# A bf16 matmul with bias and residual: load sizes of x and residual decoupled, weight loads on two queues, bias spread by a matmul

## The chip, the core and the metric

The kernel runs on one core of a Trainium2 chip. The core has five engines with queues of their own: TensorE (PE, matmul and transpose), VectorE (DVE), ScalarE (ACT), GpSimd (POOL) and SyncE (SP, which here only issues DMAs). An engine takes its instructions strictly in the order of its queue. DMAs are issued here from SP's queue and from ScalarE's, and 16 DMA engines carry them out. The metric is the device time of one execution in microseconds, lower is better.

## The reference

```python
batch, m, k, n = 16, 512, 1024, 768
# x: (16, 512, 1024), weight: (1024, 768), bias: (768,), residual: (16, 512, 768), all float32
def reference(x, weight, bias, residual):
    return (np.matmul(x, weight) + bias + residual).astype(np.float32)
```

In all 8192 rows of x are multiplied by one 1024 x 768 matrix. The kernel multiplies in bf16 and accumulates in float32. It reads 33.55 MB of x, 25.17 MB of residual and 3.15 MB of weights, and writes 25.17 MB.

## The kernel before, in words

The 8192 rows are cut into 64 row-tiles of 128 rows, counted by t. Two neighbouring row-tiles (SUB = 2) form a super s, and loads and stores go by super: one DMA brings x for 256 rows (1 MB, two rows of 4 KB, so 8 KB for each of 128 partitions), one the residual for 256 rows (768 KB), and one takes 256 rows of output away (768 KB). x, residual and output have five buffers each, so that five supers (ten row-tiles) can be in them.

Before the loop, `const` tiles are made: an identity for the transposes, the bias repeated over 128 partitions (`bias_bcast`, L102, a DMA that reads the same 3 KB for each partition), and the weights. Eight DMAs (L104), one for each slice k of 128 contraction rows, bring float32 weights into `w_stage`; VectorE casts each to bf16 in `w_sb` (L107, through the helper's L82). The bias DMA and the eight weight DMAs are all on ScalarE's queue, marked as of high priority.

A row-tile goes through these stages, each a function:

- `stage_load(s)` (L116): x and residual of a super are loaded from SP's queue (L120, L123), and GpSimd adds the bias to the residual in place (L127).
- `stage_a(t)` (L132): ScalarE casts 128 x 1024 of x to bf16 (`xb_tile`, L137 through L80). There are four such buffers.
- `stage_b(t)` (L140): TensorE transposes eight 128 x 128 blocks into PSUM (L146), VectorE copies them to `xt_tile` (L152 through L82).
- `stage_c(t)` (L155): 16 matmuls (L162), for each k one of 512 and one of 256 columns, accumulate in `psum_o`, of which there are three.
- `stage_d(t)` (L171): VectorE adds `psum_o` and the residual into `out_tile` (L176). After the second row-tile of a super, ScalarE's queue issues the store (L180).

The loop (L193) writes these down in the order load, a(t+2), b(t+1), c(t), d(t). The framework that builds the kernel puts each engine's instructions in order and inserts all waits: for data, for a buffer to come free, and for a DMA's completion semaphore to be free for use again. High priority moves instructions ahead in their queue.

Of the kernel before, what the change touches and what calls it, by code (L numbers as in the profile page):

```python
# [9 lines left out]


MM_DT = mybir.dt.bfloat16
SUB = 2
BIAS_MODE = "gpsimd"
WCV_ENGINE = "vector"
CONVERT_ENGINE = "scalar"
COPYBACK_ENGINE = "vector"
PIPE_AB = 2
X_BUFS = 5
RES_BUFS = 5  # L20
OUT_BUFS = 5
XB_BUFS = 4
XT_BUFS = 5
POUT_BUFS = 3
PTRANS_BUFS = 2
W_SPLIT = 4
W_PRIO_BUMP = 70


@with_exitstack  # L30
def kernel(
    ctx: ExitStack,
    tc: tile.TileContext,
    x: bass.AP,
    weight: bass.AP,
    bias: bass.AP,
    residual: bass.AP,
    out: bass.AP,
):
    nc = tc.nc  # L40
    P = 128
    FP32 = mybir.dt.float32
    BF16 = mybir.dt.bfloat16

    x2d = x.flatten_outer_dims()
    res2d = residual.flatten_outer_dims()
    out2d = out.flatten_outer_dims()
    M, K = x2d.shape
    Kw, N = weight.shape
    assert Kw == K  # L50
    n_k = K // P
    SUPER = SUB * P
    n_super = M // SUPER
    n_sub = n_super * SUB
    assert M % SUPER == 0

    x_sup = x2d.rearrange("(s p j) k -> s p j k", p=P, j=SUB)
    res_sup = res2d.rearrange("(s p j) n -> s p j n", p=P, j=SUB)
    out_sup = out2d.rearrange("(s p j) n -> s p j n", p=P, j=SUB)

    if N <= 512:
        n_chunks = [(0, N)]
    else:
        n_chunks = [(0, 512), (512, N - 512)]

    const = ctx.enter_context(tc.tile_pool(name="const", bufs=1))
    xin_pool = ctx.enter_context(tc.tile_pool(name="xin", bufs=1))
    xbf_pool = ctx.enter_context(tc.tile_pool(name="xbf", bufs=1))
    xt_pool = ctx.enter_context(tc.tile_pool(name="xt", bufs=1))
    res_pool = ctx.enter_context(tc.tile_pool(name="res", bufs=1))  # L70
    out_pool = ctx.enter_context(tc.tile_pool(name="outp", bufs=1))
    ptrans_pool = ctx.enter_context(tc.tile_pool(name="ptrans", bufs=1, space=bass.MemoryType.PSUM))
    pout_pool = ctx.enter_context(tc.tile_pool(name="pout", bufs=1, space=bass.MemoryType.PSUM))

    def rr_tile(pool, base, idx, nbufs, shape, dtype):
        return pool.tile(shape, dtype, name=base, tag=f"{base}{idx % nbufs}", bufs=1)

    def eng_copy(eng_name, out_ap, in_ap):
        if eng_name == "scalar":
            nc.scalar.copy(out=out_ap, in_=in_ap)  # L80
        elif eng_name == "vector":
            nc.vector.tensor_copy(out=out_ap, in_=in_ap)  # L82
        elif eng_name == "gpsimd":
            nc.gpsimd.tensor_copy(out=out_ap, in_=in_ap)
        else:
            nc.any.tensor_copy(out=out_ap, in_=in_ap)

    ident = const.tile([P, P], BF16, name="ident")
    make_identity(nc, ident)

    w_dram = weight.rearrange("(ko ki) n -> ki ko n", ki=P)
    w_sb = const.tile([P, n_k, N], MM_DT, name="w_sb")
    w_stage = const.tile([P, n_k, N], FP32, name="w_stage")

    with tc.high_priority():
        bias_bcast = const.tile([P, N], FP32, name="bias_bcast")
        bcast_ap = bass.AP(
            tensor=bias.tensor,
            offset=bias.offset,
            ap=[[0, P], bias.ap[0]],  # L100
        )
        nc.scalar.dma_start(out=bias_bcast, in_=bcast_ap)  # L102
        for k in range(n_k):
            nc.scalar.dma_start(out=w_stage[:, k, :], in_=w_dram[:, k, :])  # L104

    for k in range(n_k):
        eng_copy(WCV_ENGINE, w_sb[:, k, :], w_stage[:, k, :])  # L107

    x_tiles = {}
    res_tiles = {}  # L110
    out_tiles = {}
    xb_tiles = {}
    xt_tiles = {}
    psum_o_tiles = {}

    def stage_load(s):  # L116
        if s >= n_super:
            return
        x_tile = rr_tile(xin_pool, "x_tile", s, X_BUFS, [P, SUB, K], FP32)
        nc.sync.dma_start(out=x_tile, in_=x_sup[s])  # L120
        x_tiles[s] = x_tile
        res_tile = rr_tile(res_pool, "res_tile", s, RES_BUFS, [P, SUB, N], FP32)
        nc.sync.dma_start(out=res_tile, in_=res_sup[s])  # L123
        res_tiles[s] = res_tile
        bb = bias_bcast[:, None, :].to_broadcast([P, SUB, N])
        if BIAS_MODE == "gpsimd":
            nc.gpsimd.tensor_add(out=res_tile, in0=res_tile, in1=bb)  # L127
        else:
            nc.vector.tensor_add(out=res_tile, in0=res_tile, in1=bb)
        out_tiles[s] = rr_tile(out_pool, "out_tile", s, OUT_BUFS, [P, SUB, N], FP32)  # L130

    def stage_a(t):  # L132
        if t < 0 or t >= n_sub:
            return
        s, j = divmod(t, SUB)
        xb_tile = rr_tile(xbf_pool, "xb_tile", t, XB_BUFS, [P, K], BF16)
        eng_copy(CONVERT_ENGINE, xb_tile, x_tiles[s][:, j, :])  # L137
        xb_tiles[t] = xb_tile

    def stage_b(t):  # L140
        if t < 0 or t >= n_sub:
            return
        xb_tile = xb_tiles.pop(t)
        psum_t = rr_tile(ptrans_pool, "psum_t", t, PTRANS_BUFS, [P, n_k, P], BF16)
        for k in range(n_k):
            nc.tensor.transpose(  # L146
                out=psum_t[:, k, :],
                in_=xb_tile[:, ts(k, P)],
                identity=ident,
            )  # L150
        xt_tile = rr_tile(xt_pool, "xt_tile", t, XT_BUFS, [P, n_k, P], MM_DT)
        eng_copy(COPYBACK_ENGINE, xt_tile, psum_t)  # L152
        xt_tiles[t] = xt_tile

    def stage_c(t):  # L155
        if t < 0 or t >= n_sub:
            return
        xt_tile = xt_tiles.pop(t)
        psum_o = rr_tile(pout_pool, "psum_o", t, POUT_BUFS, [P, N], FP32)
        for k in range(n_k):  # L160
            for (n0, nl) in n_chunks:
                nc.tensor.matmul(  # L162
                    psum_o[:, n0:n0 + nl],
                    lhsT=xt_tile[:, k, :],
                    rhs=w_sb[:, k, n0:n0 + nl],
                    start=(k == 0),
                    stop=(k == n_k - 1),
                )
        psum_o_tiles[t] = psum_o

    def stage_d(t):  # L171
        if t < 0 or t >= n_sub:
            return
        s, j = divmod(t, SUB)
        psum_o = psum_o_tiles.pop(t)
        nc.vector.tensor_add(  # L176
            out=out_tiles[s][:, j, :], in0=psum_o, in1=res_tiles[s][:, j, :]
        )
        if j == SUB - 1:
            nc.scalar.dma_start(out=out_sup[s], in_=out_tiles.pop(s))  # L180

    next_load = [0]

    def ensure_loaded(s):
        while next_load[0] <= min(s, n_super - 1):
            stage_load(next_load[0])
            next_load[0] += 1

    ensure_loaded(max(1, (PIPE_AB - 1) // SUB + 1))
    for u in range(PIPE_AB):  # L190
        stage_a(u)
    stage_b(0)
    for t in range(n_sub):  # L193
        ta = t + PIPE_AB
        ensure_loaded(ta // SUB + 1)
        stage_a(ta)
        stage_b(t + 1)
        stage_c(t)
        stage_d(t)
# [30 lines left out]
```

## Time and profile before

| | us |
|---|---|
| median of 6 runs | 229.46 (229.14 to 229.60) |
| profiled execution | 229.34 |
| its span, first to last instruction | 227.6 |

| engine | busy us (share) | instructions |
|---|---|---|
| PE | 198.3 (87%) | 1536 |
| PE weight loads | 130.0 (57%) | 1536 |
| DVE | 108.9 (48%) | 136 |
| ACT | 67.8 (30%) | 65 |
| POOL | 110.7 (49%) | 38 |

The row of slices on the profile's page says how the engines' work lies over the 40 equal slices of the span, 5.69 us each: TensorE shows 0030 and then 9 until the end, the DMA engines' row shows 9 from the second slice to the 36th, then 4333. 87.68 MB were moved, 385 GB/s as a mean over the span. The granted TensorE clock was 0.994 of full speed. Transfers took, from issue to landing (medians): x 15.6 us, residual 14.9, output 8.6, weights 10.9, bias 6.8.

How to read it: a busy time is the sum of the durations of an engine's instructions; the chain of waits follows the last instruction back to what released it, step by step, and says which engine or DMA each stretch of the span belongs to. An idle time is given with a releaser, the engine or DMA whose event came last before the instruction started; where several events are waited for, the one named can be a bystander.

### The profile page before, as it was taken

The numbers are of one execution on the slowest core, as the hardware profiler recorded it, in microseconds if no ns is written. First come the engines' busy times: TensorE is split into PE (matmuls) and PEld (weight loads), VectorE is DVE, ScalarE is ACT, GpSimd is POOL, SyncE is SP. The second block draws the span as 40 slices with busy tenths as digits, with TensorE's granted clock in tenths as the row PEclk, the third lists the DMA queues.
The fourth block names the chain that finished last, engine by engine and source line by source line (L and its number), as shares of the span: only waits on it lengthen the run. The fifth ranks groups of instructions, "written<-read, shape, count | busy, mean of one in ns | idle before, by whom it ended". The sixth has DMA issues, their size and how long they took to land.

```text
span 227.6 us, 3719 instructions
## 1 busy us (share of the span) xinstructions
PE 198.3 (87%) x1536; PEld 130.0 (57%) x1536; DVE 108.9 (48%) x136; ACT 67.8 (30%) x65; POOL 110.7 (49%) x38
## 2 busy tenths in 40 slices
PE   0030499999999999999999999999999999999990
PEld 0020166666666666666666666666666666666660
DVE  0182635555444455554445555444455554444541
ACT  0080313333323333332233324233333332231000
POOL 1142876353666654165551666655555546459300
PEclk9999999999999999999999999999999999999997
DMA  6999999999999999999999999999999999994333
GB/s 202 404 407 425 415 421 343 372 419 420 424 429 419 427 419 428 424 423 426 425 423 426 419 429 420 426 422 420 425 420 427 424 421 422 425 381 185 141 140 138
DMA packets 15138, 87.68 MB, mean 385 GB/s; under 512 B 1680, under 2 KB 1680, under 8 KB 11024
## 3 DMA queue, kind: packets, MB, share of 16 engines
q1 hardware_dynamic: 9216, 58.72, 62.7%
q10 hardware_dynamic: 5904, 28.71, 30.6%
q8 instruction: 12, 0.20, 0.3%
q14 instruction: 6, 0.05, 0.1%
HBM read 62.26 MB, written 25.17 MB: 384 GB/s over the span
## 4 chain that ended last, share of the span: by engine, by line
PE 86%; DMA 9%; DVE 2%; ACTq 0%; issue 0%
PE psum_o L162 74%; PE psum_t L146 12%; DMA w_stage<-in_weight_dram 9%; DVE w_sb L82 1%; DVE out_tile L176 0%; DVE xt_tile L82 0%; ACTq L102 0%; ACTq L104 0%
## 5 line engine op out<-in xcount | busy, mean ns | idle before, releaser
L162 PE MATMUL psum_o<-w_sb,xt_tile 128*128 128x512 bf16 (+1 forms) x1024 | 178.7, 328 | 10.4 <-DVE xt_tile L82 10.4
L127 POOL TENSOR_TENSOR res_tile<-res_tile,bias_bcast 128x1536 f32<-128x1536 f32 x32 | 110.0, 3440 | 101.2 <-DMA res_tile<-in_residual_dram 91.6
L162 PEld LDWEIGHTS <-xt_tile 128*128 128x128 bf16 x1024 | 98.2, 98 | 70.1 <-DVE xt_tile L82 10.7
L176 DVE TENSOR_TENSOR out_tile<-psum_o,res_tile 128x768 f32<-128x768 f32 x64 | 61.3, 957 | 98.4 <-PE psum_o L162 56.6
L80 ACT CAST xb_tile<-x_tile 128x1024 bf16<-128x1024 f32 x64 | 66.5, 1045 | 127.0 <-PE psum_t L146 81.3
L146 PE MATMUL psum_t<-ident,xb_tile 128*128 128x128 bf16 x512 | 39.8, 222 | 13.7 <-ACT xb_tile L80 13.7
L146 PEld LDWEIGHTS <-xb_tile 128*128 128x128 bf16 x512 | 34.4, 99 | 21.9 <-ACT xb_tile L80 13.8
L82 DVE COPY xt_tile<-psum_t 128x1024 bf16<-128x1024 bf16 x64 | 43.4, 680 | 0.0
L82 DVE CAST w_sb<-w_stage 128x768 bf16<-128x768 f32 x8 | 9.4, 1184 | 16.0 <-DMA w_stage<-in_weight_dram 16.0
L80 ACT ACT_TABLE_LOAD x1 | 1.3, 1283 | 11.3 <-DMA w_stage<-in_weight_dram 11.3
masks.py:197 POOL MEMSET ident<- 128x128 bf16 x1 | 0.2, 204 | 0.3 <-POOLq L214 0.3
masks.py:199 POOL TENSOR_SCALAR_AFFINE_SELECT ident<-ident 128x128 bf16<-128x128 bf16 x1 | 0.3, 292 | 0.1
L214 POOL MEMSET const-float32-0.0<- 128x1 f32 x1 | 0.1, 98 | 0.2 <-issue 0.2
L214 POOL MEMSET const-bfloat16-1.0<- 128x1 bf16 x1 | 0.1, 102 | 0.0
L214 POOL MEMSET const-uint8-127<- 128x1 uint8 x1 | 0.1, 102 | 0.0
L214 POOL MEMSET const-float32-1.0<- 128x1 f32 x1 | 0.1, 98 | 0.0
## 6 DMA issues: line engine op xcount, KB each, us to landing
x_tile<-in_x_dram SPq DMA_DIRECT2D x32, 1024.0 KB, 15.6
res_tile<-in_residual_dram SPq DMA_DIRECT2D x32, 768.0 KB, 14.9
out_dram<-out_tile ACTq DMA_DIRECT2D x32, 768.0 KB, 8.6
w_stage<-in_weight_dram ACTq DMA_DIRECT2D x8, 384.0 KB, 10.9
bias_bcast<-in_bias_dram ACTq DMA_DIRECT2D x1, 384.0 KB, 6.8
```

What stands on the lines that cost most here:

```text
L80: nc.scalar.copy(out=out_ap, in_=in_ap)
L82: nc.vector.tensor_copy(out=out_ap, in_=in_ap)
L127: nc.gpsimd.tensor_add(out=res_tile, in0=res_tile, in1=bb)
L146: nc.tensor.transpose(out=psum_t[:, k, :], in_=xb_tile[:, ts(k, P)], identity=ident,)
L162: nc.tensor.matmul(psum_o[:, n0:n0 + nl], lhsT=xt_tile[:, k, :], rhs=w_sb[:, k, n0:n0 + nl], start=(k == 0), stop=(k == n_k - 1),)
L176: nc.vector.tensor_add(out=out_tiles[s][:, j, :], in0=psum_o, in1=res_tiles[s][:, j, :])
L214: nc = _bacc.Bacc("TRN2", target_bir_lowering=False, num_devices=1)
```

## The change

- x is loaded by four row-tiles (`XROWS` = 4: 2 MB for each DMA, 16 KB for each partition) into three buffers (12 row-tiles). The residual is still loaded by two row-tiles, now into six buffers, with counters of its own. The rows of a group of four are dealt to the partitions so that each partition holds four neighbouring rows.
- The output is stored by single row-tile: 64 stores of 384 KB in place of 32 of 768 KB, from eight buffers.
- Weight slices 4 to 7 are loaded from SP's queue with high priority, ahead of x; slices 0 to 3 from ScalarE's queue behind the bias. Casts of the weights move from VectorE to ScalarE. The matmuls take k in the order 4 to 7, 0 to 3.
- The bias is loaded as one row of 3 KB, cast to bf16, multiplied by a column of ones on TensorE (into the space of one of the `psum_o` tiles) and copied to `bias_bcast` by VectorE.
- Ahead of everything a two-element copy is put on ScalarE.

```diff
-SUB = 2
+XROWS = 4
+RES_ROWS = 2
-WCV_ENGINE = "vector"
+WCV_ENGINE = "scalar"
-X_BUFS = 5
-RES_BUFS = 5
-OUT_BUFS = 5
+X_BUFS = 3
+RES_BUFS = 6
+OUT_BUFS = 8
+W_SPLIT_ACT = 4
+K_ROTATE = 4
...
+    x_ld = x2d.rearrange("(S p j) k -> S p j k", p=P, j=XROWS)
+    res_4d = res2d.rearrange("(S p j) n -> S p j n", p=P, j=XROWS)
+    out_4d = out2d.rearrange("(S p j) n -> S p j n", p=P, j=XROWS)
...
+    k_order = [(K_ROTATE + i) % n_k for i in range(n_k)]
...
+    warm = const.tile([1, 2], FP32, name="warm")
+    nc.vector.memset(warm, 0.0)
+    nc.scalar.copy(out=warm, in_=warm)
...
     with tc.high_priority():
-        bias_bcast = const.tile([P, N], FP32, name="bias_bcast")
-        bcast_ap = bass.AP(
-            tensor=bias.tensor,
-            offset=bias.offset,
-            ap=[[0, P], bias.ap[0]],
+        for k in range(W_SPLIT_ACT, n_k):
+            nc.sync.dma_start(out=w_stage[:, k, :], in_=w_dram[:, k, :])
+
+    with tc.high_priority():
+        bias_row = const.tile([1, N], FP32, name="bias_row")
+        nc.scalar.dma_start(out=bias_row, in_=bias[None, :])
+        for k in range(W_SPLIT_ACT):
+            nc.scalar.dma_start(out=w_stage[:, k, :], in_=w_dram[:, k, :])
+
+    ones_col = const.tile([1, P], BF16, name="ones_col")
+    nc.vector.memset(ones_col, 1.0)
+    bias_row16 = const.tile([1, N], BF16, name="bias_row16")
+    nc.vector.tensor_copy(out=bias_row16, in_=bias_row)
+    bias_psum = pout_pool.tile([P, N], FP32, name="bias_psum", tag="psum_o0", bufs=1)
+    for (n0, nl) in n_chunks:
+        nc.tensor.matmul(
+            bias_psum[:, n0:n0 + nl],
+            lhsT=ones_col,
+            rhs=bias_row16[:, n0:n0 + nl],
+            start=True,
+            stop=True,
         )
-        nc.scalar.dma_start(out=bias_bcast, in_=bcast_ap)
-        for k in range(n_k):
-            nc.scalar.dma_start(out=w_stage[:, k, :], in_=w_dram[:, k, :])
+    bias_bcast = const.tile([P, N], FP32, name="bias_bcast")
+    nc.vector.tensor_copy(out=bias_bcast, in_=bias_psum)
...
+        out_tile = rr_tile(out_pool, "out_tile", t, OUT_BUFS, [P, N], FP32)
         nc.vector.tensor_add(
-            out=out_tiles[s][:, j, :], in0=psum_o, in1=res_tiles[s][:, j, :]
+            out=out_tile, in0=psum_o, in1=res_tile[:, t % RES_ROWS, :]
         )
-        if j == SUB - 1:
-            nc.scalar.dma_start(out=out_sup[s], in_=out_tiles.pop(s))
+        nc.scalar.dma_start(out=out_st_ap(t), in_=out_tile)
...
+    ensure_xloaded(0)
+    ensure_resloaded(1)
     for u in range(PIPE_AB):
         stage_a(u)
     stage_b(0)
     for t in range(n_sub):
         ta = t + PIPE_AB
-        ensure_loaded(ta // SUB + 1)
+        ensure_xloaded(ta // XROWS + 1)
+        ensure_resloaded(ta // RES_ROWS + 1)
         stage_a(ta)
         stage_b(t + 1)
         stage_c(t)
```

## The prediction

> **What bounds the kernel now.** I read the chain of waits first, then the busy shares by stretch, then the timelines of the start and of ScalarE. The chain, by line:
>
> ```profile
> PE 86%; DMA 9%; DVE 2%; ACTq 0%; issue 0%
> PE psum_o L162 74%; PE psum_t L146 12%; DMA w_stage<-in_weight_dram 9%; DVE w_sb L82 1%; DVE out_tile L176 0%; DVE xt_tile L82 0%; ACTq L102 0%; ACTq L104 0%
> ```
>
> So the run has two parts: a start that waits for the weights, and TensorE without a gap. Their border, in order of time:
>
> ```profile
> 10.80 12.21 DMA w_stage<-in_weight_dram
> 23.04 2.36 DVE w_sb L82
> 25.40 0.61 DVE xt_tile L82
> 26.05 4.79 PE psum_o L162 x16
> 30.84 0.45 PE psum_t L146 x8
> 31.29 2.60 PE psum_o L162 x16
> ```
>
> The last weight slice lands at 23.04, its cast takes 2.36, a copy 0.61, and the first output product starts at 26.05. From 31.29 each row-tile costs 2.60 + 0.45 = 3.05 us; 64 of them run to 222.37. Then come an add (0.96) and the last store, to 227.6. The stretches (columns: busy us of each engine, clock, DMA share, GB/s):
>
> ```profile
> 0.00:26.00 26.00, 1.98 (x16) 1.55 (x16) 10.00 (x10) 7.12 (x7) 7.65 (x9) 1.00 0.94 366
> ...
> 31.00:205.00 174.00, 174.00 (x1375) 114.92 (x1373) 89.02 (x115) 59.58 (x57) 91.47 (x27) 1.00 1.01 418
> 205.00:227.60 22.60, 17.34 (x128) 10.98 (x126) 9.23 (x12) 1.04 (x1) 7.49 (x3) 0.94 0.37 150
> ```
>
> TensorE is full from 31 to 205, at full clock, and **so are the DMA engines**. A row-tile moves 0.524 MB of x and 0.393 MB each of residual and output: 1.311 MB in 3.05 us is 430 GB/s, and 418 were moved. The kernel eats a stock of loaded rows all the way. An earlier start thus begins with a smaller stock.
>
> Where the stock gets short shows on ScalarE, late in the run:
>
> ```profile
> 166.29 1.05 ACT L80 CAST xb_tile<-x_tile 128x1024 bf16<-128x1024 f32 x1 [2.86 <-DVE out_tile L176]
> 168.48 1.04 ACT L80 CAST xb_tile<-x_tile 128x1024 bf16<-128x1024 f32 x1 [1.14 <-PE psum_t L146]
> 172.47 0.34 ACTq L180 DMA_DIRECT2D out_dram<-out_tile  x1
> 172.90 1.04 ACT L80 CAST xb_tile<-x_tile 128x1024 bf16<-128x1024 f32 x1 [3.38 <-DVE xt_tile L82]
> ```
>
> ScalarE stands still between 169.5 and 172.47, and the view blames VectorE, long done. The instruction records name the true cause: the 73 transfers share eight completion semaphores, and a transfer is issued only after the earlier user of its semaphore has landed. The store of 172.47 (rows 44, 45) uses that of the x load for rows 54, 55, and its count completes at 172.4. Stores at 160.13, 165.85, 178.46 and 184.60 match such landings too. So a store on ScalarE waits for x about ten rows ahead, and the casts queued behind it wait as well. TensorE feels nothing yet, since casts run six rows ahead of stores: the first store, after row 1, has eight casts before it.
>
> **The start, part by part.** The packet records give medians of 121, 234 and 309 ns for 3072, 6144 and 8192 bytes; the slope makes 16384 bytes 309 + 8192 x (75/2048) = 609 ns (estimate). Each transfer is 8 packets on each of 16 engines. In the first 12 us the two queues' packet counts run level (46 against 47 in the third and fourth us): packets alternate. That is why weights are late now: a 3 KB packet takes turns with an 8 or 6 KB one, and only five transfers of ScalarE's queue are in flight at first.
>
> *Split of the weights, ahead of x on SP.* The Trainium skill (DMA: Bandwidth & Descriptors, Issuing engines are not separate DMA queues) says that issuing on several engines saves issue time alone: four issues of 0.45 us, 1.8 us. The rows say more about this case, through order rather than rate: the slice landing at 17.6 took 1.0 us when ScalarE's queue ran alone, the one at 23.0 took 3.3 us beside x. With weights first on both queues nothing alternates with them: 64 packets per engine x 0.121 = 7.75, from the first packet at 1.75, and 1 us for the ramp (2.9 MB had moved by 10 us, about 1 us short of full rate): moved by 10.5, usable at 12.0 with 1.5 from last packet to landing. By the skill the weights would still end near 21; I take the rows.
>
> *Weight casts to ScalarE.* A 1024-element cast takes 1.045; 768 elements about 0.83 (between 0.78, in proportion, and 1.05). In slice order, five remain when slice 3 lands: 12.0 + 4.2 = 16.2. VectorE loses 9.4 us of casts off the later path, and the 2.36 on the chain with them. The early dummy copy brings the table load (1.28) forward under the weights. If x came sooner, the casts would be the wait.
>
> *x in 2 MB loads.* x0 follows the weights on SP: 8 x 0.609 = 4.87, moved at 15.4, landed at 16.9, just behind the casts. Then cast 1.05, a second cast 0.95 later to 18.9, its transposes 1.0 (the last pair took that), so **the first product starts at 20.0 instead of 26.05: 6.05 us gained**. The next x needs 1.57 MB of residual and 2.1 MB more, some 9 us: landed near 26, wanted near 30, hidden.
>
> *Bias by two matmuls, two small copies.* No row is near for one-row operands; by the 128-row ones they cost below 3 us, on idle engines behind a 3 KB load of about 3 us, with no residual before 18. Zero on the path; not below, since the broadcast load it replaces is 8 packets, 1 us of DMA, in the sum below. Rotation of k: all casts precede x, so zero. First product cold (4.79 against 2.60): kept; the transposes just before could save up to 1.5.
>
> *Granularity.* Per engine, x: 16 x 8 x 0.609 = 78.0 for 32 x 8 x 0.309 = 79.1; stores: 64 x 8 x 0.121 = 62.0 for 59.9; bias -1.0. Sum zero. Here a rule speaks against the change: the same page (Rules for kernel authors) wants 1 MiB or more per DMA, with 2.0 us fixed for each by its fit; 32 more stores would be 64 us if each paid it in line. The trace has stores in flight behind work, so only packets count: +2.1 us of DMA, inside that sum. The last store is half as long: 8 x (0.234 - 0.121) = **0.9 us gained** at the end.
>
> Without any stall: 227.6 - 6.05 - 0.9 = 220.65.
>
> **What is late next.** The store's wait for x, with a smaller stock. Seven transfers now serve four rows, so eight back is just over one round. By the buffers, x load i+4 stands after store 4i+1, hence store 4i+2 waits for x load i+3, rows 4i+12 on. Casts to row 4i+8 are already before it. The tightest is the last x load (rows 60 to 63): store 50 waits for it, cast 57 stands behind. TensorE wants that row at 192.55 (product 56 starts at 25.24 + 55 x 3.05 = 193.0), the cast must start by 191.4. The load needs per engine: weights 7.75, all x 78.0, 29 residuals 54.3, 50 stores 48.4, start and ramp 2.75, instruction fetch and semaphore packets 1.2: 192.3, landed 193.8. **Stall 2.4 us.** The same sum for the x load that landed at 172.4 gives about 174, so it leans long by under 2. Bounds: 0 (reads are served before stores) to 6 (two more rows of stock, each 3.05, wanted because four rows land at once). I take 2.4: the sum's own value.
>
> 220.65 + 2.4 = 223.05 of span. The profiled execution took 229.34, 1.74 beyond its span: 224.8; its distance to the median 229.46 is 0.12.
>
> **Rivals.**
> - *No stall, TensorE bound to the end:* 220.65 + 1.74 = 222.4. For it: large x packets against 3 KB stores give reads the DMA. Against: 418 of 430 GB/s.
> - *Slower: stores hold the casts early.* If ScalarE's queue is ordered with casts only two rows ahead of the store, as the loop is written, row 53 is the one held: 4 x 3.05 = 12.2 earlier, stall 14.6, time 237.0. It decides once the stall exceeds the 6.95 gained, so once casts stand fewer than about 4.5 rows ahead. For it: the write-up order, twice as many stores on that queue. Against: eight casts before the first store now, with the same four cast buffers.
> - *The change doesn't do what it says:* x0 waits for a semaphore or the slices come no sooner; the first product stays near 26. Then 229.34 - 0.9 = 228.4, or about 229.5 if granularity costs a us.
>
> **Numbers.** Forecast case 0.46 (its own range 222.8 to 228.4), no stall 0.24, slower 0.22, no earlier start 0.08. The range 221.8 to 232 takes the first two, most of the last and the lower part of the slower case, with about 2 in 10 outside. Faster by over 0.2% (0.46 us, about the least that can be told from no change): 0.46 + 0.24 + 0.03 = 0.73; same 0.05; slower 0.22.
>
> **What would show it.** Right: weights landed by 12, first product of L162's successor at about 20, DMA share near 1 from 4 us on; ScalarE idle before every fourth store from mid-run; a TensorE gap of 1 to 5 us around the last x loads. Wrong: no product before 25; gaps in every round of four rows (then the casts stand less far ahead); casts of weights ending after x0; stores' packets slower than 121 ns.

## The result and the profile after

The changed kernel takes 227.51 us (median of 8 runs, 226.57 to 229.77) against 229.34 for the kernel before beside it: ratio 0.9934, 95% interval 0.9902 to 0.9966. It is faster by 1.8 us where 4.6 were forecast. Some executions of a kernel are a per cent or two slower than the rest, and the first profile caught such a one (230.28 us; so did those of e1_weights_sp, 228.51, and e13_res4, 234.34, below), so the changed kernel was profiled once more (226.97 us, span 225.2; 227.63 us in the median of 10 runs, ratio 0.9925, 0.9899 to 0.9950), and the sum is read from the second profile.

The chain of waits of the first profile, one of its rows of costly groups and one of its DMA issues (count, KB each, median us to landing); behind them the same row of the kernel before, and the chain of the second profile:

```profile
PE 58%; DMA 34%; ACT 3%; issue 1%; ACTq 1%; DVE 1%; DVEq 0%
...
L90 ACT CAST xb_tile<-x_tile 128x1024 bf16<-128x1024 f32 x64 | 65.0, 1044 | 120.7 <-DMA out_dram<-out_tile 45.0
...
out_dram<-out_tile ACTq DMA_DIRECT2D x64, 384.0 KB, 13.2
...
out_dram<-out_tile ACTq DMA_DIRECT2D x32, 768.0 KB, 8.6
...
PE 67%; DMA 26%; ACT 2%; issue 1%; DVE 1%; ACTq 1%; DVEq 0%
```

Before, the DMA share of the chain was 9%, all of it weights at the start. Now it is 34% and 26% in the two profiles, and most of that is stores (27% and 20%). Stores of half the size take 13.2 us to land (11.6 in the second profile) where whole ones took 8.6, and in the first profile ScalarE stands idle 45.0 us in all before casts of x, until a store has landed.

The start, from the chain in order of time (second profile; start us, us, what):

```profile
2.65 14.16 DMA w_stage<-in_weight_dram
16.81 0.02 issue
16.83 3.76 ACT w_sb L90 x5
20.59 0.96 ACT xb_tile L90
21.55 0.05 issue
21.60 1.98 PE psum_t L176 x16
23.58 4.67 PE psum_o L192 x16
28.25 0.45 PE psum_t L176 x8
28.69 2.60 PE psum_o L192 x16
```

The last weight slice lands at 16.8, not at 12.0. Five casts follow it, as forecast, and then the cast, the transposes and the first output product. And the stretches of the second profile (columns as in the prediction):

```profile
31.00:200.00 169.00, 168.04 (x1325) 110.89 (x1324) 85.51 (x110) 57.54 (x56) 94.46 (x28) 1.00 1.01 415
200.00:225.20 25.20, 20.91 (x161) 13.41 (x158) 11.24 (x14) 3.25 (x4) 4.76 (x2) 1.00 0.52 205
```

TensorE is no longer full (168.04 of 169), while the DMA engines still are.

With starts of output matmuls taken from the instruction records (before: first 26.05, last 222.06), the 2.4 us between the spans are three terms: the first product starts at 23.42, 2.6 sooner; from the first to the last matmul it takes 197.2 in place of 196.0, 1.2 more; what follows the last is 4.6 in place of 5.5, 0.9 less.

In the table, **stall** is the time from the first to the last output matmul less 194.7, the shortest among kernels without a gap (pairs of stores). It holds gaps, and also a first product that is slower than the 3.48 us of that kernel: the kernel before has no gap, but a first product of 4.79, and so 1.3. **Landing** is as the profile's page counts it; where the bias is one row, the page has no landing for the stores on one of the eight semaphores. **Held** is the time in which ScalarE had a finished output tile to store and no other work, until the earlier user of the store's completion semaphore landed; it is worked out from the instruction and landing records, with the kind of that earlier user, over all eight semaphores. First product, stall, landing and held are of the one profiled execution; the time is the median.

| kernel | us | ratio to before (95%) | first product | stall | store landing, median / max | ScalarE held by |
|---|---|---|---|---|---|---|
| before | 229.4 | | 26.05 | 1.3 | 8.6 / 10.0 | x 27.4, residual 2.4 |
| changed, 1st profile | 227.51 | 0.9934 (0.9902 to 0.9966) | 25.15 | 4.1 | 13.2 / 19.4 | stores 61.9, x 2.7 |
| changed, 2nd profile | 227.63 | 0.9925 (0.9899 to 0.9950) | 23.42 | 2.5 | 11.6 / 21.4 | stores 49.8, x 6.4 |
| e1_weights_sp | 226.03 | 0.9833 (0.9797 to 0.9870) | 19.75 | 7.7 | 14.1 / 21.3 | stores 67.2 |
| e2_x_1mb | 227.08 | 0.9912 (0.9878 to 0.9945) | 20.69 | 5.3 | 8.7 / 12.5 | x 30.3, residual 15.0 |
| e3_store_pairs | 225.16 | 0.9819 (0.9778 to 0.9860) | 22.82 | 0 | 8.8 / 11.4 | residual 7.3 |
| e4_w_sp_pairs | 221.96 | 0.9676 (0.9638 to 0.9713) | 19.36 | 0.4 | 10.3 / 12.0 | residual 9.6 |
| e5_w_sp_x1mb_pairs | 220.86 | 0.9620 (0.9591 to 0.9649) | 17.20 | 1.8 | 8.6 / 10.0 | x 21.8, residual 4.7 |
| e6_cast_order | 225.78 | 0.9829 (0.9778 to 0.9881) | 20.12 | 5.6 | 12.6 / 19.5 | stores 58.8, x 4.4 |
| e7_pairs_3k | 237.34 | 1.0337 (1.0272 to 1.0403) | 22.93 | 10.9 | 15.1 / 22.1 | stores 3.8 |
| e9_pairs_3k_bufs | 226.71 | 0.9873 (0.9821 to 0.9926) | 24.00 | 1.0 | 17.3 / 26.8 | stores 16.9 |
| e8_halves_6k | 232.35 | 1.0115 (1.0083 to 1.0148) | 23.85 | 4.3 | 8.8 / 11.8 | x 30.5, residual 10.3 |
| e10_out16 | 225.94 | 0.9847 (0.9781 to 0.9914) | 22.89 | 3.7 | 12.4 / 20.9 | stores 60.9, x 3.2 |
| e11_xb8 | 227.43 | 0.9893 (0.9859 to 0.9926) | 22.94 | 3.5 | 11.4 / 20.3 | stores 37.8 |
| e13_res4 | 230.78 | 1.0036 (0.9995 to 1.0076) | 25.43 | 7.5 | 12.6 / 26.4 | stores 44.8 |
| e15_before_single | 228.30 | 0.9956 (0.9933 to 0.9979) | 25.78 | 2.2 | 8.9 / 13.2 | stores 22.5, x 14.2, residual 8.2 |

The time of the kernel before lay between 229.3 and 229.7 beside all of these.

### The profile page after: what moved, and what is told of

Read it like the earlier page. It is cut to its first block, busy times and chain, and to the rows that moved or that the text cites. A ratio compares the mean times of both kernels' runs of the same rounds, so it can differ in the third digit from the quotient of the medians.

```text
span 228.5 us, 3785 instructions
## 1 busy us (share of the span) xinstructions
PE 199.7 (87%) x1538; PEld 130.2 (57%) x1538; DVE 101.4 (44%) x132; ACT 72.7 (32%) x74; POOL 110.3 (48%) x38
## 4 chain that ended last, share of the span: by engine, by line
PE 58%; DMA 34%; ACT 3%; issue 1%; ACTq 1%; DVE 1%; DVEq 0%
PE psum_o L192 49%; DMA out_dram<-out_tile 27%; PE psum_t L176 9%; DMA w_stage<-in_weight_dram 7%; ACT w_sb L90 2%; ACT xb_tile L90 1%; ACTq L117 1%; DVE out_tile L207 0%; ACTq L115 0%; ACTq L210 0%; DVE xt_tile L92 0%; DVEq L207 0%; ACTq L90 0%
## 5 line engine op out<-in xcount | busy, mean ns | idle before, releaser
L90 ACT CAST xb_tile<-x_tile 128x1024 bf16<-128x1024 f32 x64 | 65.0, 1044 | 120.7 <-DMA out_dram<-out_tile 45.0
L176 PE MATMUL psum_t<-ident,xb_tile 128*128 128x128 bf16 x512 | 39.9, 222 | 21.4 <-ACT xb_tile L90 21.4
L90 ACT CAST w_sb<-w_stage 128x768 bf16<-128x768 f32 x8 | 6.3, 829 | 11.4 <-DMA w_stage<-in_weight_dram 11.4
L125 PE MATMUL bias_psum<-bias_row_101,ones_col 1*128 1x512 bf16 (+1 forms) x2 | 0.8, 499 | 3.1 <-DVE bias_row_101 L122 3.1
L133 DVE COPY bias_bcast<-bias_psum 128x768 f32<-128x768 f32 x1 | 1.0, 957 | 0.9 <-PE bias_psum L125 0.9
L122 DVE CAST bias_row_101<-bias_row 1x768 bf16<-1x768 f32 x1 | 0.5, 548 | 1.5 <-DMA bias_row<-in_bias_dram 1.5
## 6 DMA issues: line engine op xcount, KB each, us to landing
x_tile<-in_x_dram SPq DMA_DIRECT2D x16, 2048.0 KB, 15.4
out_dram<-out_tile ACTq DMA_DIRECT2D x64, 384.0 KB, 13.2
```

The costliest lines, as they stand in the source:

```text
L122: nc.vector.tensor_copy(out=bias_row16, in_=bias_row)
L125: nc.tensor.matmul(bias_psum[:, n0:n0 + nl], lhsT=ones_col, rhs=bias_row16[:, n0:n0 + nl], start=True, stop=True,)
L133: nc.vector.tensor_copy(out=bias_bcast, in_=bias_psum)
L176: nc.tensor.transpose(out=psum_t[:, k, :], in_=xb_tile[:, ts(k, P)], identity=ident,)
```

## The experiments

**The changed kernel again.**

> The changed kernel once more, for a second profile. Theory A (weights late by alternation, then a stall where a store holds the casts): first output product near 25, a TensorE gap of 1 to 4 us between 150 and 200, time 226.5 to 229. Rival (the one profile was a disturbed one): first product near 20 and no gap.

Both parts of theory A came out: a late first product (23.4; near 25 was expected) and a gap, near 190, with 227.63 us. What stops TensorE at its two gaps is not the same instruction, though. In the first profile it is a cast. ScalarE's timeline there (start us, us, what, and the idle time before it with its releaser):

```profile
170.90 0.34 ACTq L210 DMA_DIRECT2D out_dram<-out_tile  x1
171.77 1.04 ACT L90 CAST xb_tile<-x_tile 128x1024 bf16<-128x1024 f32 x1
178.62 0.34 ACTq L210 DMA_DIRECT2D out_dram<-out_tile  x1
179.05 1.04 ACT L90 CAST xb_tile<-x_tile 128x1024 bf16<-128x1024 f32 x1 [6.24 <-DMA out_dram<-out_tile]
```

TensorE's timeline at the same time, same profile and columns:

```profile
175.45 2.76 PE L192 MATMUL psum_o<-w_sb,xt_tile 128*128 128x512 bf16 x16
180.15 0.67 PE L176 MATMUL psum_t<-ident,xb_tile 128*128 128x128 bf16 x8 [1.94 <-ACT xb_tile L90]
180.61 4.44 PE L192 MATMUL psum_o<-w_sb,xt_tile 128*128 128x512 bf16 x16
```

ScalarE does nothing from 172.8 to 178.6, where it wants to store row-tile 44. That store uses the semaphore of row-tile 40's store, which was issued at 159.02 and lands at 178.5. The cast behind it comes too late and TensorE stands for 1.9 us. Its next product takes 4.44 in place of 2.76, for the granted clock reads 0.50 from 180.6 to 184.0, so that the gap costs some 1.7 us more than its own length. In the second profile:

```profile
189.55 0.61 PE L176 MATMUL psum_t<-ident,xb_tile 128*128 128x128 bf16 x8
191.13 2.77 PE L192 MATMUL psum_o<-w_sb,xt_tile 128*128 128x512 bf16 x16 [0.96 <-DVE xt_tile L92]
```

The store of row-tile 44 lands at 189.4 there, 16.8 after its issue; its buffer is wanted by the add of row-tile 52, that add waits on VectorE until 189.5, and the copy behind it comes late for TensorE. The common cause is a store that lands late.

**All weights on SP.** The edit is one constant, `W_SPLIT_ACT = 4` to `0`.

> All eight weight slices on SP's queue, ahead of x, none on ScalarE's. Theory A (the slices on ScalarE's queue start late and then alternate with 16 KB packets of x, 5.8 us a slice): last slice landed by 12, first product at 19.5 to 20.5. Rival B (the start is slow for another reason: ramp of the DMA engines, casts on ScalarE): first product stays at 24 to 26. For the time: if the end hangs on the start alone, 5 us less, near 222; if supply by DMA sets it (every transfer engine full from 50 to 200 us in the changed kernel), the earlier start is given back in longer stalls, and the time stays within 1.5 us of the changed kernel.

First product at 19.75: theory A. ScalarE's timeline shows the weights' casts and the first casts of x:

```profile
8.07 4.69 ACT L90 CAST w_sb<-w_stage 128x768 bf16<-128x768 f32 x5 [0.52 <-DMA w_stage<-in_weight_dram]
16.83 3.88 ACT L90 CAST xb_tile<-x_tile 128x1024 bf16<-128x1024 f32 x4 [4.06 <-DMA x_tile<-in_x_dram]
```

The weights' last cast ends at 12.8 and ScalarE then waits 4.06 us for x, which lands at 16.8; the forecast had 16.9. But the median gains only 1.6 us (226.03 against 227.63) where the first product comes 3.7 sooner than in the second profile. The rest goes into stall: the profiled execution, 2.5 us above the median, has 7.7, and the median would have about 5.2 with the same first product and the same end (an estimate: 226.03, less the 1.78 us between time and span, less 19.75, 194.7 and 4.55). So the end does not hang on the start alone.

The packet counts of the changed kernel (second profile) say why its own slices were late. SP's queue sends its first weight packets before 2 us; ScalarE's first slice, issued at 1.28, sends none before 3. By 9 us SP has sent nearly all of its 512 packets and begins x, while ScalarE still has some 165 of 512 to send. From 9 to 14 us the counts are 112 packets of x and 108 of weights: level again, and each x packet now takes 611 ns.

**x in 1 MB loads.** `XROWS = 4` to `2`, `X_BUFS = 3` to `6`.

> x in 1 MB loads (8 KB packets) and six buffers, all else as changed. Theory A: a slice beside x takes 3.4 us in place of 5.8, the last slice lands near 15 in place of 18.6, first product near 21.5; stores get more turns, and the store waits for two rows of x and not four, so the TensorE gap shrinks: 224 to 226. Rival (x granule makes no difference, only the store size or the total of DMA time does): first product near 25, time as changed, 227.5 within 1.

The start behaves as theory A wants (last slice 14.1, first product 20.7), and stores land in 8.7 us. The time does not follow: 227.08, with a stall of 5.3. Stores hardly wait for stores any more (0.8 us); they wait for x loads, 30.3 us, and TensorE has a gap of 2.9. That is the hold which the prediction had described, in another kernel. Eight transfers for four row-tiles use each semaphore once per round of 12.2 us.

**Stores in pairs**, the rest as changed:

```diff
...
-        nc.scalar.dma_start(out=out_st_ap(t), in_=out_tile)
+        if t % RES_ROWS == RES_ROWS - 1:
+            S, h = divmod(t // RES_ROWS, RES_PER_X)
+            nc.scalar.dma_start(
+                out=out_4d[S, :, h * RES_ROWS:(h + 1) * RES_ROWS, :], in_=out_tiles.pop(t // RES_ROWS)
+            )
```

> Stores of two row-tiles (768 KB, 6 KB packets) as in the kernel before, four such buffers, all else as changed. First product stays near 25. Theory A' (small stores are starved between 16 KB packets and their completion is what SP and ScalarE wait for): waits of SP for stores fall from 134 us to under 60, the TensorE gap goes, time 224 to 226. Rival (the wait for x on a store's semaphore alone makes the stall): gap stays, time 227 to 229, plus 0.9 at the end for the longer last store.

As A' said: SP's waits for stores drop from 134 us to 37, there is no gap, 225.16. SP's waits by the profile (us in total, times, longest), of the changed kernel and then of this one:

```profile
SPq L155 <- DMA out_dram<-out_tile: 116.9, 15, 16.1
SPq L148 <- DMA out_dram<-out_tile: 16.7, 3, 7.7
...
SPq L149 <- DMA out_dram<-out_tile: 27.1, 5, 14.5
SPq L156 <- DMA out_dram<-out_tile: 10.3, 1, 10.3
```

The chain of this kernel is TensorE's again:

```profile
PE 88%; DMA 7%; ACT 2%; DVE 0%; issue 0%
```

**Is it the packets or the count?** Pairs change both. One kernel pairs row-tiles t and t+2, which are not neighbours in memory (`out_4d[S, :, j % 2::2, :]`): half the stores, small packets. The other issues each pair of neighbours as two transfers of 64 partitions: all the stores, large packets.

> Stores of two row-tiles that are not neighbours in memory (t and t+2 of a group of four): 32 stores of 768 KB, but in 3 KB packets, so half the count of transfers with the packets of the changed kernel. Theory C (the count of transfers makes the stall: eight semaphores turn over more slowly with 5 than with 7 transfers for four rows): no TensorE gap over 1 us, time 224 to 226, as with pairs in 6 KB packets. Rival P (the 3 KB packets make it: they are starved between 16 KB packets of x): gaps of 2 to 5 us remain, time 227 to 229.

> The store of two neighbouring row-tiles in 6 KB packets, issued as two transfers of 64 partitions each: 64 transfers of 384 KB, so the count of the changed kernel with large packets. Theory C (count): gaps as in the changed kernel, 1 to 4 us, time 226.5 to 229. Rival P (packet size): no gap, 224 to 226.

Neither tells, and both are misses in time: the first has a shortage of its own (a pair stays open for three row-tiles, with four buffers; VectorE's adds wait 33 us for stores), the second a price of its own (the DMA engines are busy 217.0 us in place of 209.7, and 7.2 us follow the last product in place of 5.5). The first once more, with `OUT_BUFS = 16`:

> The kernel with 32 stores in 3 KB packets once more, with 8 double buffers in place of 4, which takes its own shortage of buffers away. Theory C (count of transfers): no gap over 1 us, 225 to 227. Rival P (small packets): stores still take 13 us or more to land and gaps of 2 us or more remain, 228 to 233.

Its row of DMA issues for the stores (count, KB each, median us to landing):

```profile
out_dram<-out_tile ACTq DMA_DIRECT2D x32, 768.0 KB, 17.3
```

Small packets stay slow (17.3 us to land, at most 26.8), and there is no gap: the stall of 1.0 is the first product, 4.50 in place of 3.48. Late stores alone don't stop TensorE, then; with 32 of them ScalarE is held for 16.9 us and with 64 for 50 to 62. It is still 1.6 us slower than pairs of neighbours; of the 2.6 us between the two profiled executions 1.2 are a later first product, 1.0 the slower one and 0.4 the end. Its buffers are twice those of the changed kernel; with the same buffers and 64 stores (next) the gaps remain, which speaks for the count. But that is one profile of each, and in time the two are not told apart (226.71 and 225.94). That pairs of neighbours cure the stall is shown; whether by their number or by their packets is not.

**Buffers and cover.** `OUT_BUFS = 8` to `16`, and `XB_BUFS = 4` to `8`, one at a time in the changed kernel.

> The changed kernel with 16 output buffers in place of 8. Theory B (small stores wait so long between 16 KB packets of x that the output buffers run out and VectorE's adds stop): adds no longer wait for stores (15 us before), gap gone, 225 to 226. Rival S (a store waits on ScalarE for its semaphore, and the casts behind it): ScalarE still waits, gap of 1 to 4 us stays, 227 to 229.

> The changed kernel with eight cast buffers in place of four, so that casts stand ten rows ahead of stores and not six. Theory S: the same wait of a store is covered by four more rows, gap gone, 224.5 to 226. Rival B (output buffers): gap stays or grows, since stores now stand behind more casts, 227 to 230.

More output buffers end VectorE's waits for stores (15.3 us to 2.0), but ScalarE is held as before and gaps of 1.2 and 1.5 us remain; its 225.9 and the changed kernel's 227.6 have intervals that overlap. More cast buffers leave a stall of 3.5 too: ScalarE now waits for x itself (59.7 us). Neither cure alone is enough, and the expectation for the second was wrong in its cause: cover for the casts is not what was short.

**Fewer other transfers.** `RES_ROWS = 2` to `4`, `RES_BUFS = 6` to `3`, one residual load at first and not two.

> The changed kernel with the residual in loads of four row-tiles (1.5 MB, three buffers): 6 transfers for four row-tiles in place of 7, the 64 small stores as they are. Theory T (stall where stores land later than the semaphores turn over): turnover 8/6 x 12.2 = 16.3 us against a landing of 12 to 14, so the gap shrinks below 1 us, time 224.5 to 226. Rival P (small stores beside 16 KB packets stall by themselves): gap of 1 to 4 us stays, 226.5 to 229.

A miss. 6 transfers in place of 7, and it is slower (230.78; its intervals and those of the changed kernel lie apart). The profiled execution, 3.6 us above the median, has a stall of 7.5 and stores that take up to 26.4 us to land. So a ratio of landing time to the semaphores' turnover, by count of transfers alone, does not carry. Residual packets are 12 KB here and take 460 ns in place of 234, which may be what stores wait for; three larger residual buffers may play a part. Neither was tried apart.

**Cast order.** `for k in k_order:` for the weights' casts.

> The changed kernel with the casts of the weights in the order in which they are multiplied, 4 to 7, then 0 to 3, so that one cast and not five follows the last slice. Last slice still lands near 17 to 18.5 (theory A); first product 3.0 us earlier, 20.4 to 22; the time gains less than 1.5, since a smaller stock lengthens the stall (with all slices on SP, 3.7 to 5.4 us of start gave 1.6 of time). Rival (the end hangs on the start): 3 less, 224.5.

First product at 20.1 (3.3 sooner than in the second profile), the time 1.9 less. The rest went into stall, which is 5.6 in the profiled execution (226.77, 1.0 above the median).

**Single stores in the kernel before**, nothing else of the change:

> The kernel before with one thing of the change alone: stores by single row-tile (64 of 384 KB, 3 KB packets, ten single buffers). x stays in 8 KB packets. If single stores alone bring a stall: slower than before, 231 to 234. If they hurt only beside 16 KB packets of x: no gap, and 0.9 less at the end, 228.5.

Here, beside x packets of 8 KB, single stores do no harm: landing 8.9, no gap, 228.30. With x in 16 KB packets the 64 stores of 3 KB packets took 11.4 to 14.1 us. Packets of 8 KB are no cure by themselves, though: x in 1 MB loads, above, had them and a gap of 2.9 us, with the first product 5 us sooner and 137 transfers, as many as here.

**Pairs and an early start together**, which the runs so far point to: pairs of neighbours with all weights on SP, and the same with x in 1 MB loads.

> All weight slices on SP's queue and stores in pairs (6 KB packets). First product at 19.5 to 20.5 as with the weights on SP alone. If pairs remove the stall for good, the 3.1 us of start are kept: 221.5 to 223. If supply by the DMA engines binds (their busy time, 209 us, cannot end earlier), part of the start comes back as gaps: 224 to 225.

> As the former, and x in 1 MB loads with six buffers. x's first load ends 2.4 us sooner, weights' casts end near 16: first product near 18.5 (1 us or so sooner). If the start is kept: 220.5 to 222; if supply binds, as the former within 1 us or slower, since x then is tied to one more transfer for every four rows (6 in place of 5).

With pairs the 3.5 us of earlier start give 3.2 of time (221.96 against 225.16), as the profiled executions also have it (first product 19.36 against 22.82, stall 0.4 against 0). The last one is the fastest of all: 220.86 us, 0.9620 of the kernel before (0.9591 to 0.9649), and its chain is TensorE's:

```profile
PE 89%; DMA 4%; SPq 2%; issue 1%; DVE 1%; ACT 0%
PE psum_o L193 76%; PE psum_t L177 13%; DMA x_tile<-in_x_dram 4%; SPq L111 2%; ACT xb_tile L90 0%; DVE out_tile L212 0%; DVE xt_tile L92 0%
```

## Why the prediction was wrong, step by step

- **The start: the step that failed is "With weights first on both queues nothing alternates with them".** The sum let the two halves of the weights run level from 1.75 us and end together at 10.5. ScalarE's half starts more than a microsecond later and has about 165 packets left when SP turns to x, each of which then waits for 611 ns of x. That is 4.8 us at the last slice (16.8 for 12.0; the working had set "near 21" against it), and 3.4 at the first product. Putting all slices on SP's queue took it away: 19.75. Why ScalarE's first slice sends so late after its issue no run told.
- **19.75 for the 20.0 of the sum is in part luck.** The casts (0.83), the 16 KB packets (611 for 609 ns) and the transposes had their size. But with all weights on SP the last weight packet ends at 11.5 and not 10.5, the last one of the first x load at 16.4 and not 15.4, and that load has landed less than 0.5 later, not 1.5. The ramp was taken too short (2.9 MB by 10 us are 1.5 us short of the working's 430 GB/s, not 1) and the landing a microsecond too long.
- **What the start was worth.** 2.8 us lie between the forecast of 224.8 and the 227.63 of the runs around the second profile. 1.6 of them go when the first product comes at 19.75 (226.03). The other 1.2 are the next two points.
- **"The store's wait for x" was the right place with the wrong holder.** ScalarE does stand at stores with casts behind them. The working let every fourth store wait, for an x load. Of the 64 stores of the changed kernel, 37 use the semaphore of an earlier store, most of them of the fourth or fifth store before, 14 that of an x load and 11 that of a residual load. A store so has about four row-tiles, 12.2 us, to land before the next one waits for it; it took 13.2 and 11.6 in the median of the two profiles and up to 21.4. ScalarE was held by stores for 61.9 and 49.8 us, by x for 2.7 and 6.4. The prediction had priced the small stores by their packets alone (+2.1 us of DMA, "only packets count") and took large x packets as a relief ("reads are served before stores"). A store's packets took the 121 ns of the working; what made them late is their turns between larger ones (8.7 to 8.9 us to land beside 8 KB packets of x, 11.4 to 14.1 beside 16 KB), and "packets alternate" stood in the working itself.
- **The stall's size.** The 2.4 of the forecast were meant on top of the kernel before, which has 1.3 in the table. On that footing the changed kernel had 1.2 in the second profile and 2.8 in the first, with first products 3.4 and 5.2 later than in the sum, so 2.5 beside 2.4 is no agreement. With the first product at 19.75 it had 6.4 in the profiled execution and about 4 in the median (by the estimate above). So the sum was too small where its own start came true, and only the late start hid that.
- **Right:** last store 0.9 forecast, 0.9 found. Casts of weights 0.829 for 0.83. Bias by matmul: `bias_bcast` is there at 4.9 us, cost zero. The slow first product: 4.67 for 4.79; in the first profile 3.50, so part of the 1.5 that the working left open. DMA sum: forecast unchanged; found 213.5 (second profile) for 213.4.
- **Two readings of the working.** The kernel before has 105 transfers on the eight semaphores; 73 is their number without the stores. And the 2.0 us for each DMA, which the working set aside, stand in the Trainium skill (DMA: Bandwidth & Descriptors, Anatomy of one DMA) as a fit for DMAs that GpSimd issues, while these stores come from ScalarE's queue. Neither entered the sum.
- **The rivals.** A stop of the casts on ScalarE was the mechanism of the slower one, with a price of 14.6; what came was between it and the forecast. That an earlier start begins with a smaller stock was shown: 3.3 to 3.7 us of start are worth 1.6 to 1.9 as long as single stores hold ScalarE, and 3.2 of 3.5 once they are pairs.

## What to carry to other kernels

In this kernel the DMA engines took turns between two queues by packet, so the size of one queue's packets set the speed of the other. Put transfers that are needed together on one queue in the order of need, and don't place small packets beside large ones unless they may be late. A DMA issued from an engine's queue can stand there until an earlier transfer with the same completion semaphore has landed, and everything behind it stands too; so count the transfers on a queue that also computes, and ask which transfer each will wait for. When the DMA engines are full, price an earlier start together with the stock that it begins with.

## What had not been expected of the hardware

A packet of 16 KB takes what the slope of the smaller ones says: 121, 234, 309 and 611 ns for 3072, 6144, 8192 and 16384 bytes. A store over 64 partitions was dear: stores of the same bytes in the same 6 KB packets, cut into two halves of the partitions, raised the engines' busy time from 209.7 to 217.0 us. The landing of a transfer is set by its slowest engine: in the second profile of the changed kernel the last of the 16 engines comes 1.8 us (median of the stores) after the eighth, and in the first one 6 us after the first at the store of 159.02, so a wait for one transfer is longer than its data took. And a gap of TensorE can cost more than its length: after gaps of 1.9 to 2.9 us in five profiles the granted clock read 0.50 for 3.4 us (changed kernel, first profile; e1_weights_sp; e2_x_1mb; e7_pairs_3k; e13_res4). One gap of 2.1 us in e1_weights_sp, and all shorter ones, were not followed by it.
